# Attention scores from one 384-column product per head pair and query chunk, added and bounded on DVE, in a Strassen-tiled transformer block

## The chip, the cores and the metric

The kernel runs on one core of one Trainium2 chip. A core has five engines with queues of their own: PE (TensorE, matrix products), DVE (VectorE), ACT (ScalarE), POOL (GpSimd) and SP (SyncE, here used to start DMAs). Products land in PSUM, which DVE and ACT can read; the other data lie in SBUF, and large intermediate arrays in DRAM. The metric is the device time of one execution in microseconds (us); lower is better. Before the change it was 897.58 us, the median of three runs (897.15 to 898.25).

## The reference

One layer of a hybrid block over a sequence of 1024 tokens of width 1024, all in float32, followed by a last RMSNorm:

```
h = rmsnorm(x, norm_g)
q, k, v, za, u, vs, zs, gm = split(h @ w_in)      # one wide input projection
q, k = partial_rope(q), partial_rope(k)           # first 16 of 64 head dims
a  = window_sink_attention(q, k, v, sinks)
a  = (a * silu(za)) @ w_att_out
sg = spatial_gating(gelu(u), gelu(vs), ...)        # 128-position blocks
sg = (sg * silu(zs)) @ w_sg_out
ga, gs = sigmoid(gm + b_merge)
x  = x + (ga * a + gs * sg) @ w_o
```

The change lies in the attention. There are 16 query heads and 2 key heads of 64 dims (8 query heads share a key head). Queries go in chunks of 64 tokens. A chunk sees its own chunk of keys and the two before it, 192 keys:

```
s = einsum(q_chunk, keys_of_window) * 64**-0.5
m = maximum(max(s), sink)          # one learned sink per head
p = exp(s - m)
denom = sum(p) + exp(sink - m)
o = (p / denom) @ values_of_window
```

## The kernel before

**Products.** Every float32 matrix is held as two parts, a high part rounded to the format that PE multiplies fast and a low part, the remainder. A product of two such matrices is three PE products (high by high, high by low, low by high). The large matrix products are tiled by Strassen's scheme: `gemm_pair` computes two row blocks of 128 rows by 1024 columns from seven products. A product (`product`, L357) is 12 matmuls of 128x128 by 512 columns, which accumulate in a PSUM bank. The seven go, in order, by the forms b11, t1, t2, b21, t3, b22 and t4. After each one `gemm_pair` calls a hook. Before some hooks `split_next` splits the weights of the next pair into high part (ACT, L176) and low part (DVE, L177); in it, once in a pair, `make_sums` forms four sums of weight blocks on DVE (L257 to L260). The results of the seven products are combined by ACT (L375, L379, L382) and DVE (L387, L392, L396).

**Attention inside the hooks.** Attention is a Python generator, `attention`, whose pieces run in the hooks of eleven pairs (three of `z_dr`, four of `gs_dr`, four of `ga_dr`). It goes through 32 steps: 2 key heads, 8 tiles of 128 tokens (two chunks each), and 2 parities of the query heads. One step handles four query heads of its key head, that is, for each of its two chunks 4 heads x 64 queries = 256 rows, in two groups of 128. A step has three parts:

- The *softmax part* (`softmax_stage`). The query tile `qt` has the high part of the queries (64 dims) on the first 64 partitions and their low part on the other 64. The key tile `kt` has the keys' high part (f = 0) and low part (f = 1), each written to both halves of the partitions. For each chunk c and group i there are two matmuls (L1433) with the same queries, one against each part of the keys, of 256 columns (128 in the first tile), which accumulate into one half of a PSUM bank; a bank holds both groups. The scores are already negated by a scale of the queries. DVE takes the minimum over the 192 keys of both groups (`TENSOR_REDUCE`, L1441) and the minimum with the negated sink (L1442). ACT takes two exponentials out of PSUM with that bound, and sums them as it goes (L1448). Then follow the sink's term (L1457 to L1459), the reciprocal (L1461) and the scaling of `pr`, half of it on DVE (L1466) and half on ACT (L1468).
- The *weight part* (`weight_stage`), for the step two earlier: six PE transposes (L1479), and the split of the result on ACT (L176, L1498) and DVE (L177, L1500).
- The *value part* (`value_stage`), for the step three earlier: four matmuls into a bank `ps_o` (L1514, L1519) and their sum on ACT and DVE (L1527, L1528); every second one writes `at_dr` to DRAM on POOL's queue (L1530).

`part_of_attention` takes `PARTS[n % 7]` parts in a hook, n being the count of hooks; in the first pair of attention it takes one. In a full pair, with W, S and V for the three kinds of parts, the parts behind the seven products are: W | S V | W | S | V | W S | V. The pools matter here: `bank("sc")` has two PSUM banks, which the softmax part uses, and `bank("o")` two, which the products by t1 and b21 share with the value part. Queries and keys of the step two later are loaded (`query_stage`, L1380, on SP's queue) behind the softmax part.

**What sets the order.** The program is written through a layer that tracks dependencies. Within an engine it takes instructions in program order, but one that it expects not to be ready yet is passed by later ones that are, by the layer's own estimate of times. So the order on an engine is fixed before the run, and can differ from the text. `after(second, first)` adds an order by hand; one such line puts the low parts of the last queries (`lows_of_q`) behind the first bounds.

Of the kernel before, what the change touches and what calls it, by code (L numbers as in the profile page):

```python
# [24 lines left out]
F32 = mybir.dt.float32  # L25
F32R = mybir.dt.float32r
AF = mybir.ActivationFunctionType
ALU = mybir.AluOpType
PSUM = bass.MemoryType.PSUM

P = 128
# [21 lines left out]
def hybrid_tile(  # L53
# [16 lines left out]
    nc = tc.nc  # L70
# [12 lines left out]
    def bank(tag, dt=F32):  # L83
        return psum.tile([P, 512], dt, name=nm("ps_" + tag), tag="ps_" + tag, bufs=2)
# [14 lines left out]
    def after(second, first):  # L99

        tc.add_manual_dep(
            second.ins,
            first.ins.name,
            mybir.DependencyInfo(mybir.DependencyClass.NoSync, mybir.DependencyReason.DATA),
            reason="order",
        )
# [464 lines left out]
    hi, lo = (g_both[0:2, n, :] for n in range(2))  # L571
# [329 lines left out]
    for c in range(2):  # L901
        hi, lo = (two_k(v, c) for v in s1_hl)
# [195 lines left out]
    bias = []  # L1098
# [122 lines left out]
    lows_of_q = []  # L1221
# [163 lines left out]
    qT = []  # L1385
# [17 lines left out]
    def atile(shape, dt, tag, bufs):  # L1403
        return mtile(shape, dt, tag, bufs, pool)

    n_pr = [0]

    def small():
        return mtile([P, 2, 2], F32, "sm", 12, aheads)
# [5 lines left out]
    def softmax_stage(g, t, par, qt):  # L1415

        kt = keys[g, t][0]
        q_of = qt[:].rearrange("p i (q c) -> p c (i q)", c=2)  # L1420
        k0 = 0 if t else P
        nmax, sums = small(), small()
        n_pr[0] += 1
        pr = mtile([P, 2, 384], F32, f"pr{n_pr[0] % 2}", 1, aheads if n_pr[0] % 2 else weights_pool)
        held_in = {}
        sinks_of = (v[:, 4 * g + par : 4 * g + par + 3 : 2] for v in (sink_sb, nsink_sb))
        sk, nsk = sinks_of
        for c in range(2):
            lo, hi = window_of(t, c)
            sc = bank("sc")[:].rearrange("p (i k) -> p i k", i=2)  # L1430
            for i in range(2):
                for f in range(2):
                    nc.tensor.matmul(  # L1433
                        sc[:, i, k0:],
                        q_of[:, c, i * P : (i + 1) * P],
                        kt[:, f, k0:],
                        start=f == 0,
                        stop=f == 1,
                    )

            nc.vector.tensor_reduce(nmax[:, c, :], sc[:, :, lo:hi], axis=mybir.AxisListType.X, op=ALU.min)  # L1441
            bound = nc.vector.tensor_tensor(nmax[:, c, :], nmax[:, c, :], nsk, op=ALU.min)  # L1442
            if n_pr[0] == 1:
                after(lows_of_q[c - 2], bound)
            for i in range(2):
                at = 192 * (1 - c) if t else P * (1 - c)
                held_in[c, i] = pr[:, i, at : at + hi - lo]
                nc.scalar.activation(  # L1448
                    held_in[c, i],
                    sc[:, i, lo:hi],  # L1450
                    AF.Exp,
                    bias=nmax[:, c, i : i + 1],
                    scale=-1.0,
                    accum_out=sums[:, c, i : i + 1],
                )
        es = small()
        nc.vector.tensor_add(es[:], sk.unsqueeze(1).broadcast_to([P, 2, 2]), nmax[:])  # L1457
        nc.scalar.activation(es[:], es[:], AF.Exp)
        nc.vector.tensor_add(es[:], es[:], sums[:])  # L1459
        inv = small()  # L1460
        nc.vector.reciprocal(inv[:], es[:])  # L1461
        for c in range(2):
            for i in range(2):
                v = held_in[c, i]
                if c == 0:
                    nc.vector.tensor_scalar_mul(v, v, inv[:, c, i : i + 1])  # L1466
                else:
                    nc.scalar.mul(v, v, inv[:, c, i : i + 1])  # L1468
        return pr

    def weight_stage(g, t, par, pr):

# [30 lines left out]
    def value_stage(g, t, par, parts):  # L1503
# [25 lines left out]
        if par == 1:  # L1529
            nc.gpsimd.dma_start(  # L1530
                at_dr[:].rearrange("(c p) t -> p c t", p=P)[:, 4 * g : 4 * g + 4, t * P : (t + 1) * P], at[:]
            )

    def attention():

        held, weights = [], []
        tiles = [step[:2] for step in steps[::2]]

        def weigh(n):
            weights.append(weight_stage(*steps[n], held.pop(0)))

        def value(n):
            value_stage(*steps[n], weights.pop(0))
            if n % 2 and n + 3 < len(steps):
                value_loads(*tiles[n // 2 + 2])

        for n, step in enumerate(steps):
            if n >= 2:  # L1550
                weigh(n - 2)
                yield
            held.append(softmax_stage(*step, qT.pop(0)))
            if n + 2 < len(steps):
                qT.append(query_stage(*steps[n + 2]))
            if n in (0, 2):
                value_loads(*tiles[n // 2])
            yield
            if n >= 3:
                value(n - 3)  # L1560
                yield
        last = len(steps)
        for n in (last - 2, last - 1):
            weigh(n)
            yield
            value(n - 1)
            yield
        value(last - 1)
        yield
# [1 line left out]
    parts = attention()  # L1571
    of_pair = [0]

    PARTS = (1, 1, 2, 1, 1, 1, 2)

    def part_of_attention(first=False):

# [596 lines left out]
```

## Time and profile before

| | |
|---|---|
| median of 3 runs | 897.58 us |
| the profiled execution | 898.48 us |
| its span, first to last instruction | 896.7 us |
| mean granted clock of PE | 0.998 |
| share of PE in the chain that ended last | 94% |
| idle time of PE from 304 to 567 us, where the scores are computed | 0.06 us |

The span is shorter than the time by what lies around the instructions. A row of the groups gives the line of the kernel, the engine, the operation, output and inputs, their shapes, the count, the summed busy time and the mean duration in ns, and after the last bar the idle time of the engine just before those instructions and what ended it. A row of a timeline gives start and duration in us, merged over neighbours of one kind (`x8`). Matmuls are pipelined, so that their durations overlap; PEld is the load of weights into PE. A row of waits reads: who waited for whom, total us, times, longest.

### The profile page before, as it was taken

The page shows a single profiled execution, that of the slowest core. Times are in us where ns is not written, and L with a number is a line of the kernel's source. Part 1 is how long each engine was busy: PE and PEld are TensorE (multiplying, and loading weights), DVE is VectorE, ACT ScalarE, POOL GpSimd, SP SyncE. Part 2 cuts the span into 40 slices and gives each one's busy share as a digit, 9 for nine tenths or more (in the row PEclk, how much of TensorE's full clock was granted, in tenths as well). Part 3 has the DMA queues.
Part 4 walks back from the last instruction along what each step waited for, and adds up shares of the span by engine and source line. Part 5 has one row for each costly group of instructions (what it writes and reads, how often), then busy time and mean ns, then how long its engine had stood idle before and what let it go on. Part 6 is the DMA issues. An engine that isn't in the chain of part 4 may idle for free.

```text
span 896.7 us, 13100 instructions
## 1 busy us (share of the span) xinstructions
PE 888.6 (99%) x4245; PEld 741.2 (83%) x4245; DVE 680.8 (76%) x1234; ACT 530.6 (59%) x1061; POOL 151.3 (17%) x218
## 2 busy tenths in 40 slices
PE   9999999999999999999999999999999999999997
PEld 6888888888888888888888888888888888888886
DVE  7879966666686788887878888647796588479986
ACT  6875523334545567767677676755585376467443
POOL 3332222212030001111110101101121121110012
PEclk9999999999999999999999999999999999999999
DMA  9998888958778768777686688899899789998633
GB/s 335 204 278 221 273 199 170 179 154 267 251 241 292 207 181 210 207 167 199 173 221 222 232 248 192 225 327 358 297 295 375 286 225 255 310 293 277 195 114 122
DMA packets 130960, 212.39 MB, mean 237 GB/s; under 512 B 12778, under 2 KB 59370, under 8 KB 130892
## 3 DMA queue, kind: packets, MB, share of 16 engines
q1 hardware_dynamic: 108280, 148.36, 49.4%
q0 software_dynamic: 22464, 62.93, 31.6%
q8 instruction: 34, 0.56, 0.3%
q14 instruction: 34, 0.28, 0.1%
q10 hardware_dynamic: 148, 0.27, 0.1%
HBM read 146.37 MB, written 86.11 MB: 259 GB/s over the span
## 4 chain that ended last, share of the span: by engine, by line
PE 94%; DMA 3%; DVE 1%; ACT 1%; issue 0%; SPq 0%; ACTq 0%
PE ps_mm L357 41%; PE ps_o L357 26%; PE ps_tp L357 7%; PE ps_sc L1433 3%; PE ps_sc L357 3%; PE ps_tp L788 2%; PE ps_tp L1479 2%; PE ps_o L788 2%; PE ps_mm L788 2%; PE ps_o L1514 2%; PE ps_tp L1104 2%; PE ps_sc L788 1%; DMA T_t1l<-in_x_dram 1%; DMA wr<-in_w_dram 1%; PE ps_o L1519 1%; DMA T_t3h<-in_w_dram 1%
## 5 line engine op out<-in xcount | busy, mean ns | idle before, releaser
L176 ACT CAST wh<-s 128x1024 fp32r<-128x1024 f32 (+1 forms) x79 | 79.3, 1006 | 84.7 <-PE ps_mm L357 39.5
L177 DVE TENSOR_TENSOR wl<-wr,wh 128x512 fp32r<-128x512 f32 (+1 forms) x77 | 72.2, 938 | 53.9 <-ACT wh L176 53.3
L177 DVE TENSOR_TENSOR wl<-s,wh 128x1024 fp32r<-128x1024 f32 (+1 forms) x79 | 92.3, 1168 | 11.5 <-ACT wh L176 11.5
L176 ACT CAST wh<-wr 128x512 fp32r<-128x512 f32 (+1 forms) x77 | 63.0, 820 | 61.0 <-PE ps_mm L357 32.8
L357 PE MATMUL ps_o<-T_t1h,wh 128*128 128x512 f32 x148 | 58.6, 396 | 0.0
L357 PE MATMUL ps_o<-T_t1h,wl 128*128 128x512 f32 x148 | 57.7, 390 | 0.0
L357 PE MATMUL ps_o<-T_t1l,wh 128*128 128x512 f32 x148 | 57.6, 389 | 0.0
L1448 ACT ACTIVATE pr<-ps_sc,sm 128x192 f32<-128x192 f32 (+2 forms) x128 | 50.8, 409 | 7.7 <-DVE sm L1442 7.2
L357 PE MATMUL ps_mm<-T_b11h,wh 128*128 128x512 f32 x140 | 54.9, 392 | 0.0
L357 PE MATMUL ps_mm<-T_t3h,wh 128*128 128x512 f32 x140 | 54.9, 392 | 0.0
L357 PE MATMUL ps_mm<-T_t2h,wh 128*128 128x512 f32 x140 | 54.7, 391 | 0.0
L357 PE MATMUL ps_mm<-T_t3h,wl 128*128 128x512 f32 x140 | 54.6, 390 | 0.0
L357 PE MATMUL ps_mm<-T_b11l,wh 128*128 128x512 f32 x140 | 54.6, 390 | 0.0
L357 PE MATMUL ps_mm<-T_t2h,wl 128*128 128x512 f32 x140 | 54.6, 390 | 0.0
L357 PE MATMUL ps_mm<-T_b11h,wl 128*128 128x512 f32 x140 | 54.6, 390 | 0.0
L357 PE MATMUL ps_mm<-T_t2l,wh 128*128 128x512 f32 x140 | 54.5, 389 | 0.0
L357 PE MATMUL ps_mm<-T_t3l,wh 128*128 128x512 f32 x140 | 54.5, 389 | 0.0
L357 PE MATMUL ps_mm<-T_t4h,wh 128*128 128x512 f32 x136 | 53.6, 394 | 0.0
L357 PE MATMUL ps_mm<-T_t4h,wl 128*128 128x512 f32 x136 | 53.2, 391 | 0.0
L357 PE MATMUL ps_mm<-T_t4l,wh 128*128 128x512 f32 x136 | 53.0, 389 | 0.0
L311 POOL DMA_DIRECT2D sums<-in_w_dram x40 | 29.3, 926 | 90.8 <-ACT x L375 42.7
L357 PE MATMUL ps_o<-T_b22h,wh 128*128 128x512 f32 x108 | 42.7, 395 | 0.0
(424 smaller groups left out, 2429.7 us busy)
## 6 DMA issues: line engine op xcount, KB each, us to landing
wr<-in_w_dram SPq DMA_DIRECT2D x86, 256.0 KB
sums<-in_w_dram POOLq DMA_DIRECT2D x20, 512.0 KB, 7.0
s<-sums SPq DMA_DIRECT2D x20, 512.0 KB
q_hl<-qhl SPq DMA_DIRECT2D x16, 512.0 KB
q<-q_hl SPq DMA_DIRECT2D x64, 128.0 KB
y_dr<-x POOLq DMA_DIRECT2D x28, 256.0 KB, 7.1
g<-in_w_dram POOLq DMA_DIRECT2D x12, 512.0 KB, 6.7
wr<-in_w_dram SPq DMA_DIRECT2D x11, 512.0 KB
```

The costliest lines, as they stand in the source:

```text
L176: hi_of.append(nc.scalar.copy(hi, src))
L177: lo_of.append(nc.vector.tensor_sub(lo, src, hi.bitcast(F32)))
L311: return lambda: paced(nc.gpsimd.dma_start(dst, src, accum_op=op))
L357: nc.tensor.matmul(acc, lt, rt, start=fresh and k == 0 and n == 0, stop=k == 3 and n == 2, skip_group_check=True,)
L788: mm = nc.tensor.matmul(acc[:], lt, rt, start=fresh and k == 0 and n == 0, stop=stops and k == 3 and n == terms[-1], skip_group_check=True,)
L1104: nc.tensor.matmul(pm[:, t * P : (t + 1) * P], xh[:, half * 4 + t, g * P : (g + 1) * P], bias[-1][1][:, g % 4, :], start=True, stop=True,)
L1433: nc.tensor.matmul(sc[:, i, k0:], q_of[:, c, i * P : (i + 1) * P], kt[:, f, k0:], start=f == 0, stop=f == 1,)
L1448: nc.scalar.activation(held_in[c, i], sc[:, i, lo:hi], AF.Exp, bias=nmax[:, c, i : i + 1], scale=-1.0, accum_out=sums[:, c, i : i + 1],)
L1479: nc.tensor.transpose(dst, pr[:, i, block * P : block * P + width], ident[:])
L1514: nc.tensor.matmul(po[:, first], va[1][:, vs], a[:, n, first], start=n == 0, stop=n == 1, skip_group_check=True)
L1519: nc.tensor.matmul(po[:, cs], vb[c][:, vs], b[c][:], start=t == 0, stop=True, skip_group_check=True)
```

## The change

- One matmul for each chunk and group takes both parts of the keys as one moving operand: 2 x 192 columns (2 x 64 and 2 x 128 in the first tile), so that the product with the high part of the keys lies in the first half of a bank and that with the low part in the second. Only the keys of the window are taken. Each group has a bank of its own, so a chunk takes both `ps_sc` banks.
- ACT copies the second half to SBUF (`sl`, two buffers). One accumulating operation of DVE adds the two halves, writes the sum to `pr`, and takes the minimum over the keys, starting from the negated sink.
- The exponential works in place in `pr`, out of SBUF.
- The softmax part becomes two parts, one for each chunk. The second holds all that follows the chunks. `held` moves out of `attention`, since `softmax_stage` is a generator now and appends to it itself.
- `PARTS` goes from (1, 1, 2, 1, 1, 1, 2) to (1, 2, 2, 2, 2, 2, 1). With Sa and Sb for the two halves, a full pair reads: W Sa | Sb V | W Sa | Sb V | W Sa | Sb | V.
- The line that ordered `lows_of_q` behind the first bounds goes.

```diff
@@ softmax_stage @@
-        k0 = 0 if t else P
...
         for c in range(2):
             lo, hi = window_of(t, c)
-            sc = bank("sc")[:].rearrange("p (i k) -> p i k", i=2)
+            wide = hi - lo
+            scores = []
             for i in range(2):
-                for f in range(2):
-                    nc.tensor.matmul(
-                        sc[:, i, k0:],
-                        q_of[:, c, i * P : (i + 1) * P],
-                        kt[:, f, k0:],
-                        start=f == 0,
-                        stop=f == 1,
-                    )
-
-            nc.vector.tensor_reduce(nmax[:, c, :], sc[:, :, lo:hi], axis=mybir.AxisListType.X, op=ALU.min)
-            bound = nc.vector.tensor_tensor(nmax[:, c, :], nmax[:, c, :], nsk, op=ALU.min)
-            if n_pr[0] == 1:
-                after(lows_of_q[c - 2], bound)
-            for i in range(2):
+                sc = bank("sc")[:, 0 : 2 * wide].rearrange("p (f k) -> p f k", f=2)
+                nc.tensor.matmul(
+                    sc, q_of[:, c, i * P : (i + 1) * P], kt[:, :, lo:hi], start=True, stop=True
+                )
+                scores.append(sc)
+            for i, sc in enumerate(scores):
                 at = 192 * (1 - c) if t else P * (1 - c)
-                held_in[c, i] = pr[:, i, at : at + hi - lo]
+                held_in[c, i] = v = pr[:, i, at : at + wide]
+                by_low = atile([P, 192], F32, "sl", 2)[:, 0:wide]
+                nc.scalar.copy(by_low, sc[:, 1, :])
+                nc.vector.tensor_tensor_reduce(
+                    v,
+                    sc[:, 0, :],
+                    by_low,
+                    1.0,
+                    nsk[:, i : i + 1],
+                    op0=ALU.add,
+                    op1=ALU.min,
+                    accum_out=nmax[:, c, i : i + 1],
+                )
                 nc.scalar.activation(
-                    held_in[c, i],
-                    sc[:, i, lo:hi],
-                    AF.Exp,
-                    bias=nmax[:, c, i : i + 1],
-                    scale=-1.0,
-                    accum_out=sums[:, c, i : i + 1],
+                    v, v, AF.Exp, bias=nmax[:, c, i : i + 1], scale=-1.0, accum_out=sums[:, c, i : i + 1]
                 )
+            if c == 0:
+                yield
...
-        return pr
+        held.append(pr)
+        yield
@@ attention @@
+    held = []
+
     def attention():
-        held, weights = [], []
+        weights = []
...
-            held.append(softmax_stage(*step, qT.pop(0)))
+            halves = softmax_stage(*step, qT.pop(0))
+            next(halves)
+            yield
+            next(halves)
...
-    PARTS = (1, 1, 2, 1, 1, 1, 2)
+    PARTS = (1, 2, 2, 2, 2, 2, 1)
```

## Prediction

> **What bounds the kernel now.** I read the page first, then the busy times of the stretch in which attention runs, then the waits of PE, then the timelines of PE, DVE and ACT over one pair of products.
>
> ```profile
> span 896.7 us, 13100 instructions
> PE 888.6 (99%) x4245; PEld 741.2 (83%) x4245; DVE 680.8 (76%) x1234; ACT 530.6 (59%) x1061; POOL 151.3 (17%) x218
> ...
> core 0: us, PE busy (x) PEld busy (x) DVE busy (x) ACT busy (x) POOL busy (x), PEclk, DMA share, GB/s
> 304.00:567.00 263.00, 262.94 (x1391) 224.40 (x1391) 214.31 (x510) 187.83 (x538) 35.87 (x46) 1.00 0.77 208
> ```
>
> The score products run from 304 to 567 us. There PE is idle for 0.06 us of 263, at the full granted clock, DVE is busy 81% and ACT 71%. So in this stage a microsecond taken from PE is a microsecond of the span, and one added to DVE or ACT costs nothing as long as PE does not wait for it. The profiled execution took 898.48 us, 0.9 above the median of 897.58; the sum is made against 898.48 and carried over to the median.
>
> **PE: what the wider product saves.** One score step (8 matmuls of 256 columns, two query chunks), a value stage behind it, and the same for a step of the first token tile, where the matmuls have 128 columns:
>
> ```profile
> 410.13 0.39 PE L357 MATMUL ps_o<-T_t1h,wl 128*128 128x512 f32 x1
> 410.36 1.11 PE L1433 MATMUL ps_sc<-k,q 128*128 128x256 f32 x8
> 411.31 0.64 PE L1514 MATMUL ps_o<-pT,v 128*128 128x512 f32 x2
> 411.78 0.40 PE L1519 MATMUL ps_o<-pTb,vb 128*128 128x256 f32 x2
> 412.02 0.40 PE L357 MATMUL ps_mm<-T_t2h,wh 128*128 128x512 f32 x1
> ...
> 436.52 1.05 PE L1433 MATMUL ps_sc<-k,q 128*128 128x128 f32 x8
> 437.41 0.68 PE L1514 MATMUL ps_o<-pT,v 128*128 128x512 f32 x2
> ```
>
> Matmuls overlap, so start-to-start spacing is the price, not the duration. Eight of 256 columns take 411.31 - 410.36 = 0.95 us, 0.119 each; two of 512 take 0.47, 0.235 each; a product's own follow at 0.23. The line through 256 and 512 columns (0.119 and 0.23) gives 0.174 for 384. A step of the changed kernel has four such: 0.70, so 0.25 less. Of 32 steps 28 are of this kind: 7.1 us. In the four steps of the first token tile eight matmuls of 128 columns take 0.89 us, 0.111 each, hardly less than those of 256. They become two of 128 and two of 256 columns: 0.46, so 0.43 less, 1.7 us for four. Together **-8.8 us**. The 128 weight loads that go have their time inside these spacings. By a rule of the Trainium skill (TensorE: Matmul & The Clock Gate, "Wait — 56ns, not 53.3ns?") a warm matmul costs its columns over 2.4 GHz plus 2.5 ns, 0.163 for 384, as an estimate; these 28 steps would then save 8.4. The trace spaces 512 columns by 0.23 where that rule has 0.216, so the rows are taken.
>
> **DVE and ACT: what is added.** Per chunk one reduction over 384 columns and one small minimum go, two adding and bounding operations over 192 columns come, each followed by a read of its accumulator. On ACT two copies out of PSUM come, and the two exponentials read SBUF.
>
> ```profile
> L630 DVE CUSTOM_DVE_ANT_0 wT<-wr 128x512 f32<-128x512 f32 x1 | 0.7, 693 | 0.4 <-DMA wr<-in_x_dram 0.4
> L630 DVE DVE_READ_ACCUMULATOR2_ANT st<- 128x1 f32 x1 | 0.1, 84 | 0.0
> L177 DVE TENSOR_TENSOR wl<-s,wh 128x1024 fp32r<-128x1024 f32 x71 | 86.8, 1222 | 11.5 <-ACT wh L176 11.5
> L1441 DVE TENSOR_REDUCE sm<-ps_sc 128x2 f32<-128x384 f32 x56 | 28.7, 553 | 1.8 <-PE ps_sc L1433 0.9
> L1442 DVE TENSOR_TENSOR sm<-sm,nsink_sb 128x2 f32<-128x2 f32 x64 | 9.3, 156 | 0.2
> L1448 ACT ACTIVATE pr<-ps_sc,sm 128x192 f32<-128x192 f32 x112 | 45.5, 419 | 2.7 <-DVE sm L1442 2.2
> L1468 ACT ACTIVATE pr<-pr,sm 128x192 f32<-128x192 f32 x56 | 22.4, 448 | 0.4 <-DVE sm L1461 0.3
> L1498 ACT CAST pTb<-ps_tp 64x256 fp32r<-64x256 f32 x60 | 22.0, 367 | 1.0
> L375 ACT COPY x<-ps_mm 128x512 f32<-128x512 f32 x23 | 13.5, 585 | 15.2 <-PE ps_mm L357 15.0
> ```
>
> The accumulating operation is in the trace once, over 512 columns: 693 ns and 84 for the accumulator. The slope of two-input DVE work, (1222 - 693) / 512 = 1.03 ns a column, gives 0.36 + 0.08 = 0.44 us for 192. Two are 0.89 against 0.553 + 0.156 = 0.71 removed: +0.18 a chunk, +10 us for 56 chunks, +1.5 by the same arithmetic for the eight narrower ones. DVE goes to at most 226 of 254 us, 89%. A copy of 192 columns lies below the 256-column cast (367) by 64 columns of the slope (585 - 367) / 256 = 0.85: 0.31 us; 112 are 35 us, 16 narrower ones some 4. An exponential out of SBUF is 29 ns dearer, the difference of the two 192-column rows: 3 us. ACT goes to at most 230 of 254, 90%. Neither passes PE, so both are priced at nothing in themselves. If that cover went, 1% more on either would cost 2.5 us.
>
> **What is on the path: the hand-over of the score banks.** There are two banks, and a half now fills both where a step did. The next half cannot start until ACT has copied and DVE has added both. From the first half to the second there is one product, 2.8 us; from there to the next first half, value stage, product and transposes, 4.0 us. After the third product of a pair (the one by t2) DVE has most to do before it reaches the scores:
>
> ```profile
> 414.79 0.82 PE L1479 MATMUL ps_tp<-ident,pr 128*128 128x128 f32 x6
> 415.36 0.47 PE L357 MATMUL ps_o<-T_b21h,wh 128*128 128x512 f32 x1
> ...
> 418.20 1.11 PE L1433 MATMUL ps_sc<-k,q 128*128 128x256 f32 x8
> ...
> 415.55 0.69 DVE L177 TENSOR_TENSOR wl<-wr,wh 128x512 fp32r<-128x512 f32 x1
> ...
> 418.55 0.69 DVE L260 TENSOR_TENSOR s<-wr,s 128x512 f32<-128x512 f32 x1
> 419.25 0.86 DVE L1500 TENSOR_TENSOR pTb<-ps_tp,pTb 64x256 fp32r<-64x256 f32 x2
> 420.14 0.69 DVE L387 TENSOR_TENSOR x<-x,ps_o 128x512 f32<-128x512 f32 x1
> 420.75 1.22 DVE L177 TENSOR_TENSOR wl<-wr,wh 128x1024 fp32r<-128x1024 f32 x1
> 421.88 1.01 DVE L1441 TENSOR_REDUCE sm<-ps_sc 128x2 f32<-128x384 f32 x2
> ```
>
> In the changed kernel a first half follows the transposes at 415.36 and ends at 415.71; the second would start after the product, at 418.55. By program order DVE works through the low parts and sums up to 420.1 before the first half's two operations, which end near 420.5 and 421.0: the banks come some 2 us late. The value stage, now at this place too, must wait for L387 to empty the other `ps_o` bank, here moved to about 421.6. The half after, L177 at 420.75 before it, is some 0.4 late and the one after the fifth product's some 1.0. After the sixth and seventh products DVE catches up. So there are four late places in each pair. What is late is not lost if the written order puts product matmuls in front. It does so in the trace: this value stage stands inside the product by t3 (first three rows), and beside it is the one place where scores already wait for their banks:
>
> ```profile
> PEld ps_o L1514 <- DVE x L387: 0.4, 1, 0.4
> ...
> 574.77 0.39 PE L357 MATMUL ps_mm<-T_t3l,wh 128*128 128x512 f32 x1
> 575.16 0.73 PE L1514 MATMUL ps_o<-pT,v 128*128 128x512 f32 x2
> ...
> 575.97 0.39 PE L357 MATMUL ps_mm<-T_t3h,wl 128*128 128x512 f32 x1
> ...
> 307.98 1.32 PE L1433 MATMUL ps_sc<-k,q 128*128 128x128 f32 x8
> 309.14 0.44 PE L357 MATMUL ps_mm<-T_t2h,wh 128*128 128x512 f32 x1
> ```
>
> The first took 575.97 - 574.77 = 1.20 where 0.23 + 0.71 (the value stage at 411.31) is the price unhindered: 0.26 lost. The second took 1.16 against 0.89: 0.27 lost. A late place so costs about 0.265 us if the order foresees it, nothing if it foresees it perfectly, and the whole 2 us if it does not. I take two waits a pair, since a wait gives DVE the same time to catch up and the four places are one backlog: 2 x 0.265 x 10 full pairs = **+5.3 us**. The ends are 0 and 4 x 0.265 x 10 = +10.6.
>
> **Edits taken at nothing.** Each step has one part more (128 for 96) and seven hooks now take 12 parts for 9, so the number of products crossed stays; the last value stage falls behind the last product, 0.7 us of PE work that is merely moved. The dropped order of the first bounds behind the query's low parts can cost one wait of 0.27. Loads of queries, keys and values are issued after the second half, some 3.5 us later on SP's queue; the weight loads and stores behind them wait as they did:
>
> ```profile
> SPq L1380 <- PE ps_sc L1433: 31.0, 13, 4.3
> at_dr<-aT POOLq DMA_DIRECT2D x14, 256.0 KB, 3.5
> ```
>
> A query has two steps, 17 us, to arrive. A transfer of twice its size lands in 3.5 here, so the remaining 13 hide it; uncovered, each late microsecond would be PE's. On ACT an exponential that waits for DVE holds casts of weights for the next pair, a product or more ahead of their use.
>
> Sum: -8.8 + 5.3 = **-3.5 us**, 895.0 by the profiled execution, **894.1** as a median.
>
> **Rivals.** *The hand-over waits in place* (slower). If PE's written order doesn't move the late halves, or DVE comes later on the chip than that order supposes, PE stands at the fourth product of each pair. At 2.0 us in 10 pairs this is +20 - 8.8 = +11.2, 908.8; at 1.6 a pair, 904.8. It decides from 0.88 us a pair. For it: DVE and ACT at 90% and steps in series (copy, add, exponential) where both chunks went together. Against it: the value stage moved into the product above. The Trainium skill (TensorE: Matmul & The Clock Gate, "Step-by-step: what each phase is for") says that only weight loads are pulled ahead and matmuls stay in program order, which would make the rest of the queue stand too; the 1.16 us at 307.98 agree.
> *All is hidden*: 888.8, if the waits foreseen are exact. For it: PE idle 0.06 us in 263. Against: both placements above lost time.
> *They cancel*: some three to four waits a pair, within 1.8 us of 897.6.
> *The wide product isn't cheaper*: if 384 columns in two pieces went at the rate of the 128-column rows (0.111 / 128 a column, 0.333), a step would cost 1.33 instead of 0.95: +0.38 x 28 - 1.7 = +8.9, 906.5. Against: 512 columns go at 0.23.
>
> **Chances.** 0.2% (1.8 us) is about what this measurement tells from none. Partial gain (889.8 to 895.7, my forecast) 0.39; all hidden 0.08; cancel 0.13; hand-over waits in place 0.36; wide product no cheaper 0.04. Faster 0.47, same 0.13, slower 0.40. The bounds of my own terms reach from 888.8 to 899.4; for 8 in 10 the range takes in the slower rival up to 1.6 us a pair: 889 to 905.
>
> **What would show it.** PE's score rows: four of 384 columns in about 0.70 us a step. Busy DVE near 89% and ACT near 90% in the stage. Waits of PE on L1433's banks, named ACT or DVE, two per pair and 0.2 to 0.3 each; halves standing inside the t3 and b22 or t4 products. One long wait per pair at the second half behind b21 would prove the slower rival; score rows spaced 0.24 or more, the last one. The prediction is wrong if idle PE in the stage exceeds 8 us, or if it stays below 1.

## The result

| | before | after |
|---|---|---|
| median | 898.2 us (897.15 to 898.49, 5 runs) | 902.02 us (901.43 to 902.66, 5 runs) |
| span of the profiled execution | 896.7 us | 899.6 us |
| granted clock of PE | 0.998 | 0.998 |
| share of PE in the chain that ended last | 94% | 77% |

The changed kernel is slower: the ratio is 1.0046, with a 95% interval of 1.0031 to 1.006. The prediction was 894.1 us, faster. The time lies in its range of 889 to 905, on the wrong side of no change.

The page of the changed kernel: the span, the busy times, and the engines' shares of the chain that ended last; then the busy times of the same stretch as before.

```profile
span 899.6 us, 13022 instructions
PE 885.8 (98%) x4117; PEld 731.1 (81%) x4117; DVE 686.9 (76%) x1362; ACT 562.2 (62%) x1189; POOL 152.9 (17%) x218
PE 77%; DVE 9%; ACT 5%; DMA 4%; issue 3%; SPq 1%; POOL 0%; ACTq 0%; DVEq 0%
```

```profile
304.00:567.00 263.00, 257.54 (x1240) 210.76 (x1239) 213.62 (x613) 211.94 (x644) 35.11 (x45) 1.00 0.74 201
```

PE was idle for 0.06 us of this stretch before, and is idle for 5.46 now. DVE and ACT are busy 81% of it, far from full. The chain has moved in part from PE to DVE and ACT. The waits of PE, and of its weight loads, on the score banks:

```profile
PE ps_sc L1433 <- DVE sm L1442: 4.9, 13, 0.9
PEld ps_sc L1433 <- DVE sm L1442: 14.7, 25, 1.0
```

Before there was next to nothing of the kind. The two rows mustn't be added: 12 of PE's 13 waits are places at which its weight load waits too, so these are 26 places and not 38. What a place costs is read from the starts of the matmuls, as the spacing beyond the undisturbed one (0.228 us for 512 columns, 0.176 for 384, 0.118 for 256, 0.109 for 128, worked out from the timelines). The 26 places cost 12.3 us: one in the first pair of attention 1.1, and 25 in the ten full pairs 0.14 to 0.83 each, 0.45 in the mean. Ten of the 25 stand in the product by t3, nine in that by t4, six at the end of that by t1.

The whole of attention is read from the starts of the product by b11: its eleven pairs run from 301.55 to 585.33 us before, and from 300.59 to 588.26 after. That is 283.8 against 287.7 us, 3.9 more. (They begin 1.0 us earlier, for a reason that wasn't looked into; behind them the two kernels take the same time, and the spans differ by 2.9.) With every matmul at its undisturbed spacing the eleven pairs would take 281.0 us before and 272.6 after, 8.4 less, close to the 8.8 of the prediction. So the wide products do save their time, but what the matmuls take beyond these spacings rose from 2.8 to 15.1 us. That is 12.3 us, the cost of the 26 places.

The groups that the change makes, counted over the whole execution:

```profile
L1433 PE MATMUL ps_sc<-k,q 128*128 128x384 f32 x112 | 38.5, 385 | 3.7 <-DVE sm L1442 3.1
L1441 ACT COPY sl<-ps_sc 128x192 f32<-128x192 f32 x112 | 29.4, 312 | 0.0
L1442 DVE CUSTOM_DVE_ANT_0 pr<-ps_sc,sl,nsink_sb 128x192 f32<-128x192 f32 x112 | 42.2, 414 | 15.4 <-ACT sl L1441 14.5
L1442 DVE DVE_READ_ACCUMULATOR2_ANT sm<- 128x1 f32 x128 | 10.6, 83 | 0.0
L1452 ACT ACTIVATE pr<-pr,sm 128x192 f32<-128x192 f32 x112 | 50.1, 448 | 21.3 <-DVE sm L1442 21.0
```

The last column of each shows who now waits: DVE 14.5 us for ACT's copies, ACT 21.0 us for DVE's sums. One such place, the second half behind b21, in a pair that starts at 402.33 us; first PE, then the weight load of the same matmul, then DVE:

```profile
418.22 0.39 PE L357 MATMUL ps_mm<-T_t3l,wh 128*128 128x512 f32 x1
418.94 0.45 PE L1433 MATMUL ps_sc<-k,q 128*128 128x384 f32 x1 [0.32 <-DVE sm L1442]
419.22 0.39 PE L357 MATMUL ps_mm<-T_t3h,wl 128*128 128x512 f32 x1
419.45 0.34 PE L1433 MATMUL ps_sc<-k,q 128*128 128x384 f32 x1
419.63 0.39 PE L357 MATMUL ps_mm<-T_t3h,wh 128*128 128x512 f32 x1
```

```profile
418.93 0.19 PEld L1433 LDWEIGHTS ps_sc<-k,q 128*128 128x128 f32 x1 [0.74 <-DVE sm L1442]
```

```profile
417.56 0.86 DVE L1502 TENSOR_TENSOR pTb<-ps_tp,pTb 64x256 fp32r<-64x256 f32 x2
418.45 0.42 DVE L1442 CUSTOM_DVE_ANT_0 pr<-ps_sc,sl,nsink_sb 128x192 f32<-128x192 f32 x1
418.80 0.41 DVE L1442 CUSTOM_DVE_ANT_0 pr<-ps_sc,sl,nsink_sb 128x192 f32<-128x192 f32 x1
419.14 0.68 DVE L387 TENSOR_TENSOR x<-x,ps_o 128x512 f32<-128x512 f32 x1
```

The written order did move the half into the product by t3, but not far enough. The product's matmul at 418.22 should have been followed at 418.45. The score matmul comes at 418.94, 0.49 late, when DVE has added the bank's content at 418.45 to 418.87. Undisturbed it takes 0.18 (419.45 to 419.63), here 0.28, so this place lost 0.59. The product's own matmuls stand behind it; that agrees with the Trainium skill (TensorE: Matmul & The Clock Gate, "Step-by-step: what each phase is for"), by which matmuls stay in program order.

### The profile page after: what moved, and what is told of

The parts are those of the page before. It is cut to its first block, busy times and chain, and to the rows that moved or that the text cites. A ratio compares the mean times of both kernels' runs of the same rounds, so it can differ in the third digit from the quotient of the medians.

```text
span 899.6 us, 13022 instructions
## 1 busy us (share of the span) xinstructions
PE 885.8 (98%) x4117; PEld 731.1 (81%) x4117; DVE 686.9 (76%) x1362; ACT 562.2 (62%) x1189; POOL 152.9 (17%) x218
## 4 chain that ended last, share of the span: by engine, by line
PE 77%; DVE 9%; ACT 5%; DMA 4%; issue 3%; SPq 1%; POOL 0%; ACTq 0%; DVEq 0%
PE ps_mm L357 34%; PE ps_o L357 19%; PE ps_tp L357 7%; PE ps_sc L357 3%; PE ps_tp L788 2%; PE ps_o L788 2%; PE ps_mm L788 2%; DMA wr<-in_w_dram 2%; PE ps_sc L1433 2%; PE ps_tp L1104 2%; ACT pr L1452 1%; DVE pr L1442 1%; DVE pTb L1502 1%; PE ps_sc L788 1%; PE ps_tp L1481 1%
## 5 line engine op out<-in xcount | busy, mean ns | idle before, releaser
L1452 ACT ACTIVATE pr<-pr,sm 128x192 f32<-128x192 f32 (+2 forms) x128 | 55.9, 439 | 24.2 <-DVE sm L1442 23.9
L1442 DVE CUSTOM_DVE_ANT_0 pr<-ps_sc,sl,nsink_sb 128x192 f32<-128x192 f32 (+2 forms) x128 | 46.7, 401 | 16.7 <-ACT sl L1441 15.8
L1433 PE MATMUL ps_sc<-k,q 128*128 128x384 f32 (+2 forms) x128 | 42.7, 376 | 5.5 <-DVE sm L1442 4.9
```

The costliest lines, as they stand in the source:

```text
L1433: nc.tensor.matmul(sc, q_of[:, c, i * P : (i + 1) * P], kt[:, :, lo:hi], start=True, stop=True)
L1442: nc.vector.tensor_tensor_reduce(v, sc[:, 0, :], by_low, 1.0, nsk[:, i : i + 1], op0=ALU.add, op1=ALU.min, accum_out=nmax[:, c, i : i + 1],)
L1452: nc.scalar.activation(v, v, AF.Exp, bias=nmax[:, c, i : i + 1], scale=-1.0, accum_out=sums[:, c, i : i + 1])
```

## The experiments

Each run was timed in five rounds beside the kernel before, on the same chip. "Without hand-over" means that the copies and the adding operations, unchanged in number and size, read a tile of zeros in SBUF; the scores are left out of the result in all such runs, and a copy takes 344 ns in e1 where it took 312 out of PSUM.

| run | what it is | us | ratio to before (95%) |
|---|---|---|---|
| e1 | after, without hand-over | 899.17 | 1.0005 to 1.0023 |
| e2 | after, ACT alone empties the banks | 904.96 | 1.0062 to 1.0088 |
| e3 | before's products in after's parts | 905.84 | 1.0077 to 1.0104 |
| e4 | after, DVE adds earlier | 899.86 | 1.0013 to 1.003 |
| e5 | e1, value part one hook later | 897.92 | 0.999 to 1.0008 |
| e6 | e3, value part one hook later | 903.9 | 1.005 to 1.0075 |
| e7 | after, value part one hook later | 903.49 | 1.005 to 1.0075 |
| e8 | e4 with other parts | 901.13 | 1.0023 to 1.0048 |
| e9 | after, sums on GpSimd | 907.9 | 1.0104 to 1.0136 |
| e10 | before, sums on GpSimd | 899.21 | 1.0006 to 1.0023 |
| e11 | e1, sums on GpSimd | 908.2 | 1.0096 to 1.0148 |
| e12 | e3, sums on GpSimd | 913.22 | 1.015 to 1.0177 |
| e13 | after, scores and value part later on PE | 899.52 | 1.0012 to 1.0032 |
| e14 | e3, value part later on PE | 903.91 | 1.0057 to 1.0082 |
| e15 | e1, value part later on PE | 897.56 | 0.9987 to 1.0006 |
| e16 | the wide product, but one part a step | 898.93 | 1.0001 to 1.0019 |
| e17 | e16 without hand-over | 903.38 | 1.0049 to 1.0074 |
| e18 | e16, second chunk's products later on PE | 897.16 | 0.9984 to 1.0002 |

### Is it the hand-over of the banks? (e1, e2)

The prediction's slower rival says so. e1 takes the hand-over away and leaves all the work; e2 lets ACT copy the whole bank, so that the bank no longer waits for DVE.

```diff
-                nc.scalar.copy(by_low, sc[:, 1, :])
+                nc.scalar.copy(by_low, zeros[:, 0:wide])
...
-                    sc[:, 0, :],
+                    zeros[:, 0:wide],
```

> The changed kernel, with ACT's copies and DVE's adding operations reading a constant tile in SBUF in place of the scores (the scores are left out of the result); number and size of all instructions stay. Theory A (the hand-over of the two score banks costs PE what the wide product saves): nothing waits for the banks, so the whole saving shows: 8.8 us under before, 889 to 891, idle PE in the score stage under 0.5 us. Theory B (the wide product or the new places of the parts cost PE time themselves): 895 or more with no idle PE. Theory C (DVE or ACT have become the bound by their load of some 81 to 85%): 900 or more, since their work is unchanged.

```diff
-                nc.scalar.copy(by_low, sc[:, 1, :])
+                nc.scalar.copy(both, sc)
...
-                    sc[:, 0, :],
+                    both[:, 0, :],
```

> ACT copies both parts of the scores (384 columns) to SBUF, and DVE adds and bounds from there, so that ACT alone frees a bank and DVE's queue is off the hand-over; ACT gets some 0.17 us more per copy, 19 to 22 us in all. Theory A with DVE as the late engine: the waits behind b21 and b22 go for the most part, idle PE falls from 5.5 us in the stage to under 2, the time to 893 to 897. Theory A with ACT as the late engine, or theory C for ACT: 902 or more, with waits now put down to ACT.

e1 is 2.9 us faster than after, and still slower than before, although PE has 8 to 9 us less to do and waits for no bank of scores. That is the time of theory B, but not its sign, since PE does wait, on PE's row and on that of its weight loads for the same thing at the same places (so that the sums of 16 to 20 us in later expectations count each place twice):

```profile
PE ps_o L1518 <- DVE x L387: 6.6, 9, 1.0
PEld ps_o L1518 <- DVE x L387: 10.8, 10, 1.4
```

PE now waits for L387, DVE's sum of the product by b21 into `x`, which empties the `ps_o` bank that the value part takes (the other one holds the product by t1, to which that by b22 is still added). There is one such wait in each full pair, and by the starts of the matmuls the ten cost 9.5 us. e2 is slower than after, as its second theory had it: the weight loads of the scores wait for ACT instead of DVE (12.0 us, 33 times), and those of the value part for L387 too (6.1 us, 9 times). So the hand-over is one of two waits, and when it goes the other shows.

### Is it the number of parts? (e3, e16)

e3 has the products, reductions and exponentials of before and only the split into parts by chunk, with the new `PARTS`. e16 is the opposite: the wide product, copies and adding operations in one part a step, with the old `PARTS`.

```diff
@@ e3: on before @@
+            if c == 0:
+                yield
...
-    PARTS = (1, 1, 2, 1, 1, 1, 2)
+    PARTS = (1, 2, 2, 2, 2, 2, 1)
@@ e16: on after @@
-            if c == 0:
-                yield
...
-    PARTS = (1, 2, 2, 2, 2, 2, 1)
+    PARTS = (1, 1, 2, 1, 1, 1, 2)
```

> The kernel before, its products and reductions kept, with each query chunk a part of its own and the changed numbers of parts per hook. Theory A: a chunk fills one bank of two, so there is a bank to spare at each hand-over; 897 to 899, idle PE under 1 us. Theory B (the places cost time by themselves, for instance the value part directly behind b21): 900 to 902.

> The wide product, the copy and the adding operation alone, without the part per chunk: both chunks in one part, at the places of the kernel before. Then the second chunk's two products always need the banks of the first at once, and the order puts 70 of the 128 score products inside the big products. If the hand-over of the banks is what costs (theory of the prediction), more places are late than in the changed kernel: 902 to 912. If the splitting into more parts is the greater cost (parts alone cost 7.7), this comes out below the changed kernel, 893 to 900.

e3 costs 7.7 us with no new work at all, more than either theory had. So the parts by chunk, which the prediction took at nothing, are a cost of their own: 7.7 us without the wide product, and 3.1 with it (902.0 to 898.9). The wide product without them, e16, costs 1.0 net; as it also has the saving of 8.4, it loses 9 to 10 us, at places where PE waits for the score banks and some where it waits for L387. So neither cost is the whole, and the two don't simply add up to the 12.3 of the changed kernel. The wait in e3 is again that on L387:

```profile
PEld ps_o L1517 <- DVE x L387: 10.0, 10, 1.9
```

DVE's order has a part in it. In the kernel before, DVE takes the reduction of the scores behind L387 (420.14 and 421.88 in the prediction's rows), since the scores behind b21 are the next to come. With parts by chunk a first half stands behind t2, a product earlier, and its reduction (or its two adding operations) is written in front of L387, as in the rows of after above and in these of e3, from DVE's timeline:

```profile
419.43 0.56 DVE L1441 TENSOR_REDUCE sm<-ps_sc 128x2 f32<-128x384 f32 x1
419.91 0.68 DVE L387 TENSOR_TENSOR x<-x,ps_o 128x512 f32<-128x512 f32 x1
```

Measured from the first matmul of b21, as a mean over the ten full pairs (worked out from the timelines):

| | end of L387 | start of the value part behind that end |
|---|---|---|
| before | 5.38 us | 0.89 us |
| e3, parts alone | 5.63 | 0.05 |
| e6, e3 with the value part one hook later | 6.18 | 0.26 |
| e1, without hand-over | 6.02 | 0.06 |
| after | 5.90 | 0.27 |
| e16, one part a step | 6.51 | 0.10 |
| e18, one part, later places | 6.92 | 0.05 |

A value of 0.05 is a value part that starts at once when L387 is done: it was waiting. The kernel before has 0.89 us in hand at this place in the mean (0.06 in the last pair). One of its pairs:

```profile
421.88 0.62 PE L1514 MATMUL ps_o<-pT,v 128*128 128x512 f32 x2
```

L387 was through at 420.83. Each of the two edits uses that up. The copy and the adding operation make L387 1.1 us later (e16). The parts make it only 0.25 later in e3, but they also bring the value part forward: before, it stands mostly behind the 12th matmul of t3 and starts 6.27 us behind the first of b21, and in e3 it stands mostly behind the 9th and would have started at 4.96 without the wait. With its old place behind the 12th (e6, below) L387 itself is 0.8 later than before, and nine of ten value parts start within 0.41 us of it.

### Another place, another order (e4 to e8)

e4 orders DVE by hand: two sums of weight blocks and the low parts of `pTb` go behind the first half's adding operations. e5 to e8 change `PARTS` so that the value part behind b21 moves a hook on (e5 to e7), or spread the parts otherwise (e8).

```diff
@@ e4 @@
+                    while behind_scores[i]:
+                        after(behind_scores[i].pop(), added)
@@ e5, e6, e7 @@
-    PARTS = (1, 2, 2, 2, 2, 2, 1)
+    PARTS = (1, 2, 2, 2, 1, 3, 1)
@@ e8 @@
-    PARTS = (1, 2, 2, 2, 2, 2, 1)
+    PARTS = (2, 2, 2, 2, 1, 2, 1)
```

> The changed kernel, with DVE's order changed by hand: the low parts of the second group of transposes and two of the four sums of weight blocks stand behind the adding operations of the first half in the same hook. Theory A with DVE's place in the queue as the cause: after the product by t2 the banks come 1 to 2 us sooner, the waits behind b21 (0.25 to 0.73 us each) go, 897 to 899. If the adding operations are late because ACT's copies are late, nothing is won: 901 to 903.

> The kernel without hand-over (copies and adding operations read a constant tile, the scores are left out of the result), with the value part of the fourth hook moved to the fifth (1, 2, 2, 2, 1, 3, 1). Theory D (two causes: the score banks, and a value part behind b21 that waits for the ps_o bank until DVE has done L387): with both taken away the whole saving shows, 889 to 891, no waits of PE on L387. If the wide product or the many parts cost PE time in some other way: 894 or more without PE waits.

> The kernel before with a part per chunk, the value part of the fourth hook moved to the fifth. Theory D: the 7.7 us that the parts cost alone came from the value part behind b21; 897 to 899, no idle PE. If a part per chunk costs time itself: 902 to 906.

> The changed kernel with the same move of the value part. In the changed kernel the second half of the scores, which stands in the product by t3 and waits for DVE, comes ahead of the value part, so the bank of L387 is free by then. Theory D with the score banks as what binds in the changed kernel: 900 to 903. If the place of the value part is what the changed kernel lost: 892 to 896.

> The changed kernel with DVE's adding operations ahead of late low parts and sums (as in the run with that change alone), the value part at the fifth hook, and the third step's halves behind the sixth and seventh products (2, 2, 2, 2, 1, 2, 1), so that fewer scores stand inside a product (18 for 49 in the changed kernel). Theory D: both causes are smaller, 893 to 897, under the kernel before. If the score banks bind wherever the halves stand: 899 to 902.

e4 gains 2.2 us over after, short of the 3 to 5 expected, with the score banks' waits of the weight loads at 9.6 us in place of 14.7; but the value part now waits for L387 (3.6 us, 10 times). e5 gains 1.3 over e1, where theory D had 8 to 10, and e6 1.9 over e3, which is its second expectation. In both the value part still waits (e5: 7.1 us, 9 times; e6: 6.9 us, 8 times), though on PE it now stands behind the 12th matmul of t3 in place of mostly the 10th (e1) and the 9th (e3). In e7 it waits no more, and the banks do, so that it loses 1.5 against after. e8 is slower than e4, as its second theory had it. Moving a wait by a hook doesn't do away with it.

### Less work on DVE (e9 to e12)

If DVE is late at this place, relieving it there should help. The four sums of weight blocks, 2.4 us of DVE in each pair, go to GpSimd.

```diff
@@ make @@
+            if of_hook[0]:
+                for dst, one, two in ((s1, a21, a22), (s2, s1, a11), (s3, a11, a21), (s4, a12, s2)):
+                    nc.gpsimd.tensor_tensor(dst, one, two, op=ALU.add)
+                return
```

> The changed kernel with one edit: in the attention stage the four sums of weight blocks of each pair of products (L257 to L260, 2.4 us of DVE a pair) are taken by GpSimd instead of DVE. Theory D (what is lost is lost behind DVE's backlog after the product by t2: the adding operations come late there, and the banks with them): DVE is 2.4 us a pair earlier at the second halves, the waits on the score banks (19.6 us in all in the changed kernel, some 9 of them real) fall to about a third, and the time to 891 to 897. Theory H (the two banks alone: PE waits for a hand-over of copy, add and semaphores whenever two score rows stand close, however free DVE is): the waits stay at 15 to 20 and the time at 900 to 903. If GpSimd's sums (some 1.5 us each, 6 us a pair) come too late for the products that read them, a new wait of PE on L257 to L260 shows instead, and the time says nothing of the two.

> The kernel before with the same edit alone, as the control: its PE waits for next to nothing, so both theories expect 897 to 899 here. Slower than 900 would say that GpSimd's sums are late or slow DVE down by themselves, faster than 896 that the kernel before already loses time behind DVE.

> The changed kernel without the hand-over of the score banks (copies and adding operations read a constant tile; the scores are left out of the result) and with the four sums on GpSimd. Without the second edit it took 899.2, with waits of 17 us on DVE's sum x of the layer (L387) before the value part. Theory D: these waits go too, and the saving of the wide products shows in full, 889 to 892. If the places of the parts cost PE time by themselves, whatever DVE does, it stays at 896 to 899.

> The products of the kernel before, in parts by query chunk as in the changed kernel, with the four sums on GpSimd. Without the second edit it took 905.8, with waits of 16 us on L387 before the value part. Theory D: these waits go, and it comes to 897 to 900, the time of the kernel before. If splitting the stage into more parts costs PE time by itself, it stays at 903 to 906.

All got slower, the control e10 by 1.3 us, and the others by 6 to 9, beyond every time expected of them. As a test of DVE's load they don't count, for two reasons. The first is in the timelines of e10: a GpSimd sum, a scaling of `pr` on DVE beside it, and one without a sum beside it.

```profile
432.73 1.28 POOL L260 TENSOR_TENSOR s<-wr,wr 128x512 f32<-128x512 f32 x1 [1.23 <-DVE sm L1464]
```

```profile
414.86 0.55 DVE L1471 TENSOR_SCALAR pr<-pr,sm 128x192 f32<-128x192 f32 x2
432.97 2.42 DVE L1471 TENSOR_SCALAR pr<-pr,sm 128x192 f32<-128x192 f32 x2
```

Two scalings take 2.42 us instead of 0.55 when GpSimd adds at the same time. All seven pairs of scalings of this size in e10 that met a sum took 2.4 to 2.5. The Trainium skill (SBUF — State Buffer, "Terms") says that DVE and GpSimd share a pair of ports, and that one holds it for a whole instruction while the other stands still; these rows agree. The second reason is that the planner, with less on DVE, wrote the scores and the value part earlier on PE (in e12 the value part behind the 2nd matmul of t3, in e3 behind the 9th), where they wait again. GpSimd took work from DVE and gave the time back in blocked instructions, so the question stayed open.

### Are the written places too early? (e13, e14, e15, e18)

The order on PE is fixed ahead by estimated times. These runs hold a score product or the value part to a later matmul of a product, so that PE has work in front of it.

```diff
@@ e13; in e14 and e15 only the value part, in e18 the second chunk's products @@
+                for score, at in of_scores:
+                    if 3 * k + n + 1 == at:
+                        after(score, mm)
...
+                place = {4: 11, 6: 8}.get((of_pair[0] - 1) % 7 + 1)
+                if c == 1 and i == 0 and of_pair[0] > 7 and place:
+                    later_scores.append((score, place))
```

> The changed kernel; only the written order of PE differs: the second half behind b21 is held to the 11th matmul of the product by t3 (before: 8th), the value part to its end (11th or 12th), and the second half behind b22 to the 8th of the product by t4 (5th). Theory P (the order is fixed ahead from estimated times, and the estimates are some tenths of a microsecond early, wherever DVE or ACT in truth are later; what is lost is the difference, and work of PE put in front would fill it): the waits in those two products (0.25 to 0.73 and 0.03 to 0.53 each) go, 894 to 898 in place of 902. Theory R (the lateness is handed on: a later half frees its banks later, and the next half and what follows wait instead): the waits stand elsewhere, 900 to 903.

> The products of the kernel before in parts by query chunk (905.8 in an earlier run, with ten waits on L387 of 1.0 to 1.9 before the value part, which stands behind the 9th matmul of t3), with the value part held to the end of t3. Theory P: each of the ten waits loses the three matmuls put in front, 0.69: 898 to 900. Theory R: DVE is late by as much more, 903 to 906. If DVE is late by the softmax tail on ACT, the rest of the wait (0.3 to 1.0 a pair) stays on L387 in either case.

> The changed kernel without the hand-over of the banks (constant tile in the place of the scores, so that they are left out), 899.2 in an earlier run with ten waits on L387 before the value part behind the 10th matmul of t3; here the value part is held to the end of t3. Theory P: two matmuls in front, 0.46 of each of ten waits: 893 to 896. Theory R: 898 to 900.

> The product alone without a part per chunk (898.9), with the products of the second chunk held two matmuls of PE later (0.46 us) at each of its three places a pair, where they waited for the banks 0.42 us on average, 21 times. If the waits go and nothing is handed on, 3 to 7 us go: 892 to 896, faster than both kernels. If lateness is handed on as in the run with later places (of 5 expected 2.4 came), 896 to 898. If the banks bind in a loop, 898 to 900.

e13 comes to 899.52, 2.5 us less than after; e14 gains 1.9 over e3, e15 1.6 over e1, e18 1.8 over e16. (e14 puts the value part where e6 has it, behind the 12th matmul, and takes the same time, so the two are one result.) The expectation for places that are merely too early was 4 to 8, 6 to 8, 3 to 6 and 3 to 7. So part of the loss is a place some tenths too early, and the larger part stays. The waits of the weight loads in e16 and then in e18 show it handed on:

```profile
PEld ps_sc L1433 <- DVE sm L1442: 8.9, 21, 1.1
PEld ps_o L1514 <- DVE x L387: 2.8, 9, 0.7
```

```profile
PEld ps_sc L1440 <- DVE sm L1452: 1.2, 4, 0.6
PEld ps_o L1524 <- DVE x L394: 6.3, 10, 1.5
```

(L394 is L387 in e18's numbering.) The banks' waits went from 8.9 to 1.2 us, and those for L387 grew from 2.8 to 6.3. e18, the best of all versions, is at 897.16 against 897.76 of the kernel before: not to be told from no change.

### What is left without either? (e17)

e17 is e16 without hand-over: one part a step, no bank waits, the copies and adding operations still there.

```diff
@@ on e16 @@
-                nc.scalar.copy(by_low, sc[:, 1, :])
+                nc.scalar.copy(by_low, zeros[:, 0:wide])
...
-                    sc[:, 0, :],
+                    zeros[:, 0:wide],
```

> The product alone without a part per chunk, as in the run before, and without the hand-over of the banks: copies and adding operations of the same size read a constant tile, so that the scores are left out of the result. The order is that of the kernel before (16 score rows a pair less, all at the 12th matmul). Theory C (the parts per chunk make DVE and ACT wait for each other twice a step, in queues that go in order, and PE waits for what comes late of that; it is this and not the added 53 us of DVE and ACT work that kept the saving from showing in the runs without hand-over): with one exchange a step the saving of the wide products shows in full, 889 to 892. Theory L (the added work of DVE and ACT is the cause): as with the parts, 896 to 899.

It came out at 903.4, beyond both expectations, and so isn't a clean test. Rows of its timeline of PE and DVE, and one of its waits:

```profile
416.25 0.50 PE L357 MATMUL ps_o<-T_b21h,wh 128*128 128x512 f32 x1
419.15 1.03 PE L1435 MATMUL ps_sc<-k,q 128*128 128x384 f32 x4
420.01 0.39 PE L357 MATMUL ps_mm<-T_t3h,wh 128*128 128x512 f32 x1
422.53 0.39 PE L357 MATMUL ps_mm<-T_t3h,wl 128*128 128x512 f32 x1
422.95 0.73 PE L1516 MATMUL ps_o<-pT,v 128*128 128x512 f32 x2
```

```profile
414.65 0.42 DVE L1444 CUSTOM_DVE_ANT_0 pr<-zeros,sl,nsink_sb 128x192 f32<-128x192 f32 x1 [0.96 <-ACT sl L1443]
417.62 0.69 DVE L177 TENSOR_TENSOR wl<-wr,wh 128x512 fp32r<-128x512 f32 x1
422.21 0.69 DVE L387 TENSOR_TENSOR x<-x,ps_o 128x512 f32<-128x512 f32 x1
```

```profile
PEld ps_sc L1435 <- PE ps_sc L1435: 5.2, 27, 0.2
```

Four products in a row go through two banks, and the third waits for the first although nobody reads it: 0.86 us (419.15 to 420.01) where four spacings of 0.176 are 0.70. Over 28 steps that is, as an estimate, 4.5 us of the run's own making. The rest is informative. DVE stood 0.96 us waiting for ACT's copy, which on ACT's queue comes behind the first chunk's exponentials. Its low part of the weights starts 1.37 us after b21 (417.62 - 416.25), against 0.19 in the kernel before (415.55 - 415.36), and L387 is 1.2 us later by the same count (422.21 - 416.25 = 5.96 against 420.14 - 415.36 = 4.78). The value part waits for it, 0.19 us beyond its place. So the chain of copy, sum and exponential, which goes twice to and fro between two queues in order, delays what stands behind it on DVE even where no bank is handed over. How much of the loss would remain without the parts and without the hand-over can't be said: about 899 if the 4.5 us are taken off, which is an estimate.

## Why the prediction was wrong

**The scores' products: right.** A product of 384 columns that waits for nothing takes 0.17 to 0.18 us to the next start (419.45 to 419.63 above), as the line through 256 and 512 columns said. Of the 8.8 us forecast, 8.4 are in the starts of the matmuls.

**The added work: priced at nothing, which the runs don't bear out.** The copy took 312 ns (forecast 0.31), the exponential out of SBUF 448 (0.448). The adding operation took 414 and 83 where 0.36 and 0.08 were forecast, but two follow at 0.35 (418.45 to 418.80), so a chunk pays less than that. ACT rose by 31.6 us over the execution (forecast 42), DVE by 6.1 (forecast 11.5), and neither came near the 89 and 90% of the stage that were named as a sign. "Neither passes PE, so both are priced at nothing in themselves" doesn't follow: they are busy 81% and still late, while they wait for each other (DVE 14.5 us for copies, ACT 21.0 for sums). That this exchange is what makes them late is argued from the timelines; no run takes it away alone. In the stretch, ACT's exponentials wait for DVE like this, in before and in e14, which has before's operations in more parts:

```profile
ACT pr L1448 <- DVE sm L1442: 7.2, 6, 3.4
```

```profile
ACT pr L1455 <- DVE sm L1449: 60.3, 36, 3.2
```

**The hand-over: the step that failed.** The term was two waits a pair at 0.265 us, in ten full pairs: +5.3, and at most +10.6. Measured are 25 waits in the ten full pairs at 0.45 us, 11.2 us, and one of 1.1 us in the first pair, for which the sum had nothing: 12.3 us. The number was nearly right: in nine of the ten pairs one in the product by t3 and one in that by t4, and in six pairs one by t1. Whether for the reason given, that "a wait gives DVE the same time to catch up", no run shows. The price of one was wrong by a factor of 1.7. It came from two places of the kernel before that lost 0.26 and 0.27 us, and nothing showed that a late half in the changed kernel would be foreseen as well as those were. With 12.3 in the place of 5.3, and 8.4 in that of 8.8, the forecast of 3.5 us faster turns into the 3.9 slower that were measured in attention. The places can't be mended one by one either: held later, the halves wait less, and the value part waits for L387 (e18, and in part e13).

**"Edits taken at nothing": the second failure.** One part more per step was called free because the number of products crossed stays. e3 prices it at 7.7 us alone, and taking it out of the changed kernel (e16) wins 3.1. It brings the reduction or the sums in front of L387 on DVE, and the value part to an earlier place on PE, where 0.89 us were in hand. The prediction saw that the value part "must wait for L387", but counted that into the same backlog.

**The rivals.** The slower one, waits in place of the saving, is what happened in direction, and 1.1 us a full pair is beyond the 0.88 from which it was to decide. Its form was another: not one long wait of 1.6 to 2.0 us a pair at the second half behind b21, but two or three of 0.14 to 0.83. That the time lies in the range is owed to this rival, for which the range was widened, and not to the sum. The halves do stand inside the products by t3 and t4, as forecast. The test set for the prediction, idle PE in the stage between 1 and 8 us, was a bad one: 5.46 us lie inside it although the direction was wrong. Idle time leaves out the first 0.16 us of each wait, in which the 0.39 us of the matmul before still count as busy though the next was due after 0.23. It also leaves out that a matmul behind a wait takes longer itself, and the waits that come after the stretch.

What remains open is the floor: no run shows the saving of the wide product in full as a faster kernel, and none separates the exchange between ACT and DVE from the sheer number of instructions in front of L387. No run gives the scores or the value part a third bank either.

## What to carry to other kernels

Two engines that are each busy 80% are not free if they take turns: count how often they hand something to each other in a step, and what stands behind each turn in their queues. Before moving work, measure how much time is in hand at the tightest place (here 0.89 us between L387 and the value part) and compare it with what the edit puts in front of it, in that order of instructions. A price taken from two places that happen to be late in the old kernel (0.265 us) isn't the price of such places in the new one (0.45). And price a change that only regroups work by a run of its own: here the split alone cost 7.7 us, though it adds no work.

## What the runs showed of the hardware

- GpSimd's `tensor_tensor` over SBUF blocks DVE: two scalings of `pr` took 2.42 us instead of 0.55 beside it. The adding operation of e9, which reads PSUM and one SBUF tile, stayed at 0.41 beside the sums; that of e11, which reads two SBUF tiles, took up to 1.44.
- Two matmul groups written one after the other to the same bank waited for each other in e17, with no reader between: four products through two banks took 0.86 us instead of 0.70. Whether the chip needs that wait or the layer only puts it there, no run shows.
- A matmul behind a wait takes about 0.1 us longer itself: 0.28 us to the next start (418.94 to 419.22) instead of 0.18, and likewise at the other places that wait in after.
